# Weight tiles 32 bytes apart and gated features staggered by 16 bytes, in a two-layer hybrid trunk on one core

## The chip, the core and the metric

The kernel runs on one core of a Trainium2 chip. The metric is the device time of one execution in microseconds: the median of several runs. All matrix work is done by TensorE (PE), whose operands both come from SBUF: a *stationary* operand of 128 columns, brought in by a weight load (PEld), and a *moving* operand, streamed past it column by column. VectorE (DVE), ScalarE (ACT) and GpSimd (POOL) do the rest, SyncE (SP) issues the loads.

## The reference, cut to what matters

Two layers, each a mixer (differential attention, latent attention, a state space branch, three gates) and a gated feed-forward network, on 512 tokens of 1024 features in fp32. Nearly all arithmetic is in products like these:

```python
proj = h @ w_in[l]                       # 1024 x 8112
merged = ga * (ya @ w_branch_a[l]) + gb * (yb @ w_branch_b[l]) + gc * (ys @ w_branch_c[l])
x = x + g_m * (merged @ w_out[l])
u = _causal_dwconv(h @ ffn_w_up[l], ffn_conv_w[l], ffn_conv_b[l])   # 1024 x 5632
ua, uv = jnp.split(u, 2, axis=-1)
x = x + g_f * ((jax.nn.silu(ua) * uv) @ ffn_w_down[l])              # 2816 x 1024
```

## The kernel before, in words

Every large product is computed from split operands. A factor is written as a high part, rounded to the matmul's fp32r type, and a low part, the remainder; three matmuls (high with high, high with low, low with high) add up in PSUM. `mm3` (line 140) is that triple: line 141 has the high weights stationary and the high features moving, line 142 the same weights and the low features, line 143 the low weights and the high features. So the weights that are loaded are high, high, low, and so on.

Weights arrive by DMA as a raw tile `wr` of four blocks of 128 rows by 256 columns (1024 fp32 numbers in each partition). `split` (line 126) makes the high part `wh` on ScalarE (line 132) and the low part `wl` on VectorE (line 133), each in a tile of 1024 numbers. The pool `wp` holds three buffers each of `wr`, `wh` and `wl`, so weights are prepared up to some groups ahead. Some groups take `wh` and `wl` from other pools (`wo`, `wd`, `wx`), where a stage needs more of them at once.

`feat_groups` (line 156) is the usual loop: for four blocks of rows at a time it prepares the weights and then issues 4 x 2 triples, two blocks of 128 output features side by side, each over all 512 tokens. `feat_halves` does the same with the tokens in two halves of 256, for the stretches where a norm sits between two products. `tok_groups` (line 192) turns the roles round: the features are stationary and the weights move, 256 columns at a time (lines 220 to 222).

The moving or stationary features are `hh`, `hl` (normed input of a stage, 8 blocks of 512 tokens each), `yh`, `yl` (branch outputs), `mh`, `ml` (merged branches) and `gh`, `gl` (gated features of the feed-forward network, line 1437). In `Ffn.run` (line 1424) the up-product is computed in two parts, of 12 and 10 blocks of 128 features. For each block the gated value `u` is split into `gh` and `gl`, tiles of 512 numbers out of 13 buffers each; then the down-product runs over the blocks of that part with `gh`, `gl` as the moving operand, the second part partly in halves.

The order of the instructions on each engine comes from the program's own order and a scheduler, and the change leaves it as it is on all five. What the pools decide besides the waits is where a tile lies: a pool is laid out tile after tile along the partition, and a tile's length sets where the next begins.

Of the kernel before, what the change touches and what calls it, by code (L numbers as in the profile page):

```python
# [10 lines left out]
F32R = mybir.dt.float32r  # L11
# [7 lines left out]
P = 128  # L19
S = 512  # L20
# [45 lines left out]
def trunk_kernel(ctx: ExitStack, tc: tile.TileContext, a: dict, out: bass.AP):  # L66
# [4 lines left out]
    wp = ctx.enter_context(tc.tile_pool(name="wp", bufs=3, reuse_waits="tile"))  # L71
# [52 lines left out]
        return raw  # L124

    def split(raw, n, scales=None, pool=None):
        hi = (pool or wp).tile([P, 1024], F32R, name="wh")
        lo = (pool or wp).tile([P, 1024], F32R, name="wl")
        for o, m, col in scales or ((0, n, None),):
            sl = slice(o, o + m)  # L130
            if col is None:
                nc.scalar.activation(hi[:, sl], raw[:, sl], AF.Copy)  # L132
                nc.vector.tensor_tensor(out=lo[:, sl], in0=raw[:, sl], in1=hi[:, sl], op=ALU.subtract)  # L133
            else:
                nc.scalar.activation(hi[:, sl], raw[:, sl], AF.Copy, scale=col)
                nc.vector.scalar_tensor_tensor(out=lo[:, sl], in0=raw[:, sl], scalar=col, in1=hi[:, sl],
                                               op0=ALU.mult, op1=ALU.subtract)
        return hi, lo
# [17 lines left out]
    def feat_groups(w, cols, nk, rhs, evac):  # L156
# [5 lines left out]
        def group(k0):  # L162
            n = min(4, nk - k0)

            def prep():
                rows = w[k0 * P:(k0 + n) * P, :].rearrange("(k p) c -> p k c", p=P)
                if joined:
                    raw = load([(0, (n, 256), rows[:, :, cols[0]:cols[0] + 256])])
                    view = "p (k i c) -> p i k c"
                else:  # L170
                    raw = load([(i * n * P, (n, P), rows[:, :, c:c + P]) for i, c in enumerate(cols)])
                    view = "p (i k c) -> p i k c"
                wh, wl = split(raw, n * 256)
                bg(2)
                return [x[:, 0:n * 256].rearrange(view, k=n, i=2) for x in (wh, wl)]

            def mm(weights):
                vh, vl = weights
                if k0 == 0:
                    st["banks"] = [mbank(), mbank()]  # L180
                for k in range(n):
                    xh, xl = rhs(k0 + k)
                    for i in range(2):
                        mm3(st["banks"][i], vh[:, i, k], vl[:, i, k], xh, xl, k0 + k == 0, k0 + k == nk - 1)
                    if k0 + k == nk - 1:
                        for i in range(2):
                            evac(i, st["banks"][i])
                    yield 1.28
            return prep, mm
        return [group(k0) for k0 in range(0, nk, 4)]  # L190

    def tok_groups(w, segs, hh, hl, evac):
# [5 lines left out]
        def group(half):  # L198
            def prep():
                rows = w[half * 512:(half + 1) * 512, :].rearrange("(k p) c -> p k c", p=P)  # L200
                raw = wp.tile([P, 1024], F32, name="wr", bufs=3)
                rv_, off = raw[:, 0:4 * width].rearrange("p (k c) -> p k c", k=4), 0
                for c, n in segs:
                    nc.sync.dma_start(out=rv_[:, :, off:off + n], in_=rows[:, :, c:c + n])
                    off += n
                return split(raw, 4 * width)

            def mm(weights):
                wh, wl = weights
                if half == 0:  # L210
                    st["banks"] = [mbank().rearrange("p (t c) -> p t c", t=2) for _ in range(2)]
                for t in range(T):
                    bank = st["banks"][t // 2]
                    o = bank[:, t % 2, 0:width]
                    ts_ = slice(t * P, (t + 1) * P)
                    first, last = half == 0 and t % 2 == 0, half == 1 and t % 2 == 1
                    for k in range(4):
                        kk = 4 * half + k
                        sl = slice(k * width, (k + 1) * width)
                        nc.tensor.matmul(o, hh[:, kk, ts_], wh[:, sl], start=first and k == 0, stop=False)  # L220
                        nc.tensor.matmul(o, hh[:, kk, ts_], wl[:, sl], start=False, stop=False)  # L221
                        nc.tensor.matmul(o, hl[:, kk, ts_], wh[:, sl], start=False, stop=last and k == 3)  # L222
                    if last:
                        evac(t // 2, bank)
                    yield 1.28
            return prep, mm
# [4 lines left out]
    def feat_halves(w, cols, nk, rhs, evac, joint, pool=None, spare=0):  # L231


        st = {}

        def prep():
            out = []
            for k0 in range(0, nk, 4):
                n = min(4, nk - k0)
                raw = load([(0, (n, 256), w[k0 * P:(k0 + n) * P, cols[0]:cols[0] + 256].rearrange("(k p) c -> p k c", p=P))])  # L240
                out.append([x[:, 0:n * 256].rearrange("p (k i c) -> p i k c", k=n, i=2) for x in split(raw, n * 256, None, pool if nk - k0 <= 4 * spare else None)])
            return out

        def mm(weights, h):
            if h == 0 or not joint:
                st["banks"] = [mbank(), mbank()]
            for k in range(nk):
                vh, vl = weights[k // 4]
                xh, xl = rhs(k)
                for i in range(2):  # L250
                    o = st["banks"][i][:, HALF[h]]
                    mm3(o, vh[:, i, k % 4], vl[:, i, k % 4], xh[:, HALF[h]], xl[:, HALF[h]], k == 0, k == nk - 1)
                if k == nk - 1 and not (joint and h == 0):
                    for i in range(2):
                        if joint:
                            evac(i, st["banks"][i])
                        else:
                            evac(i, st["banks"][i][:, HALF[h]], HALF[h])
                yield 0.64
        return prep, mm  # L260
# [91 lines left out]
    def lin_feat(*args):  # L352
        run_groups(feat_groups(*args))
# [388 lines left out]
    def mix(l, x, hh, hl, ckr, cq, latp, scope):  # L742
# [258 lines left out]
        with ExitStack() as att:  # L1001
# [210 lines left out]
            for h in range(2):  # L1212
                for nm in ("qn", "kn"):
                    mla_transpose(0, h, nm)
            fill(MLA_HEAD[1])
            run(units, events, lambda u: MLA_FILL[u // 8] * MLA_SHAPE[u % 4], (2, 3))
            fill()
            yb = []
# [176 lines left out]
    class Ffn:  # L1395
# [28 lines left out]
        def run(self, fp, extra):  # L1424

            l, x = self.l, self.x
            last = []
            for p0, p1 in ((0, 12), (12, NPAIR)):
                gs = []
                for p2 in range(p0, p1, 2):  # L1430
                    for side in range(2):
                        if (p2, side) != (0, 0):
                            lin_feat(*self.up_args(p2, side))
                    for i in range(2):
                        u = self.us[0, i]
                        nc.vector.tensor_tensor(out=u, in0=u, in1=self.us[1, i], op=ALU.mult)
                        gh = fp.tile([P, S], F32R, name="gh", bufs=13)
                        gl = fp.tile([P, S], F32R, name="gl", bufs=13)
                        nc.scalar.activation(gh, u, AF.Copy)
                        nc.vector.tensor_tensor(out=gl, in0=u, in1=gh, op=ALU.subtract)  # L1440
                        gs.append((gh, gl))
                for n2 in range(4):
                    def evac(i, bank, sl=slice(0, S), n2=n2):
                        n = 2 * n2 + i
                        nc.vector.scalar_tensor_tensor(out=x[:, n, sl], in0=bank, scalar=mod[l][:, 40 + n:41 + n], in1=x[:, n, sl],
                                                       op0=ALU.mult, op1=ALU.add)
                    args = (a["ffn_w_down"][l][p0 * P:p1 * P, :], (n2 * 256, n2 * 256 + P), p1 - p0, lambda k, gs=gs: gs[k], evac)
                    if p0 == 0 or n2 < 2:
                        lin_feat(*args)
                    else:  # L1450
                        last.append(feat_halves(*args, False, extra, 3 * (n2 - 2)))
            return last
# [72 lines left out]
    for l in range(DEPTH):  # L1525
# [13 lines left out]
        fp = np_scope.enter_context(tc.tile_pool(name=f"ffn{l}", bufs=1, reuse_waits="tile"))  # L1539
# [41 lines left out]
```

## Time and profile before

| | |
|---|---|
| time, median of 3 runs (lowest to highest) | 2087.01 us (2086.53 to 2087.76) |
| the profiled execution: its own time | 2087.19 us |
| its span in the profile | 2085.2 us |
| PE busy | 2060.7 us (99% of the span) |
| DVE, ACT, POOL busy | 1415.1, 923.4, 136.0 us |
| HBM traffic | 113 GB/s over the span |

The profile has about 2 us less than the execution's own time: what lies before the first and after the last instruction. A matmul's record begins when it starts and lasts longer than the time to the next one, since matmuls are pipelined: of two successive records the starts tell the pace, and the records' own length does not. A weight load runs beside the matmul before the one that it is for.

### The profile page before, as it was taken

How to read it: one execution, taken by the hardware profiler on the slowest of the kernel's cores; microseconds unless marked ns; L12 is line 12 of the kernel's file. 1: busy time of each engine (PE TensorE's matmuls, PEld its weight loads, DVE VectorE, ACT ScalarE, POOL GpSimd, SP SyncE). 2: the span in 40 equal slices, each digit the busy share in tenths (PEclk: the TensorE clock that was granted, in tenths of full speed). 3: DMA queues.
4: the chain of work that ended last, by engine and by line, in shares of the span. 5: the costliest groups of instructions: out<-in, count | busy, mean ns of one | idle time of the engine just before them, and what ended most of it. 6: DMA issues, size and time to landing. Idle time of an engine off the chain costs nothing.

```text
span 2085.2 us, 30158 instructions
## 1 busy us (share of the span) xinstructions
PE 2060.7 (99%) x11469; PEld 1794.4 (86%) x11469; DVE 1415.1 (68%) x2731; ACT 923.4 (44%) x1702; POOL 136.0 (7%) x162
## 2 busy tenths in 40 slices
PE   8999999999999999999999999999999999999999
PEld 7889988899888988888898888889998888888888
DVE  7788887747876778657767887765566566553553
ACT  6744445535533444224344544454444334432431
POOL 4200011002100000000000000110020000000000
PEclk8999999999999999999999999999999999999999
DMA  8523232243455265655443222212333242323322
GB/s 268 154 61 92 71 117 86 86 123 105 143 157 171 85 189 171 193 175 159 156 136 91 71 61 88 64 48 79 95 89 93 91 132 91 101 91 96 97 91 81
DMA packets 224542, 237.20 MB, mean 114 GB/s; under 512 B 16126, under 2 KB 195742, under 8 KB 224142
## 3 DMA queue, kind: packets, MB, share of 16 engines
q1 hardware_dynamic: 221646, 232.63, 36.5%
q0 software_dynamic: 2752, 2.65, 0.5%
q8 instruction: 90, 1.47, 0.3%
q14 instruction: 54, 0.44, 0.1%
HBM read 226.30 MB, written 8.91 MB: 113 GB/s over the span
## 4 chain that ended last, share of the span: by engine, by line
PE 85%; DVE 5%; issue 5%; DMA 2%; POOL 1%; ACT 1%; SPq 0%; POOLq 0%; DVEq 0%; ACTq 0%
PE mb L141 20%; PE mb L142 20%; PE mb L143 20%; PE mb L220 3%; PE mb L222 3%; PE mb L221 3%; PE ab L1168 2%; PE mb L662 1%; PE ab L1136 1%; DMA wg<-in_ada_w_dram 1%; DVE wl L133 1%; PE ab L961 1%; DVE macc L518 1%; PE ab L1319 1%; PE ab L1078 1%
## 5 line engine op out<-in xcount | busy, mean ns | idle before, releaser
L141 PE MATMUL mb<-hh,wh 128*128 128x512 f32 (+1 forms) x1376 | 538.5, 392 | 2.9 <-DVE modsum L530 1.4
L143 PE MATMUL mb<-hh,wl 128*128 128x512 f32 (+1 forms) x1376 | 532.9, 387 | 0.0
L142 PE MATMUL mb<-hl,wh 128*128 128x512 f32 (+1 forms) x1376 | 532.5, 387 | 0.0
L133 DVE TENSOR_TENSOR wl<-wr,wh 128x1024 fp32r<-128x1024 f32 (+2 forms) x312 | 375.2, 1204 | 201.2 <-ACT wh L132 195.5
L132 ACT ACTIVATE wh<-wr 128x1024 fp32r<-128x1024 f32 (+2 forms) x312 | 324.5, 1041 | 337.3 <-PE mb L142 257.4
L141 PEld LDWEIGHTS mb<-hh,wh 128*128 128x128 f32 x1376 | 258.6, 188 | 53.4 <-DVE modsum L530 2.6
L143 PEld LDWEIGHTS mb<-hh,wl 128*128 128x128 f32 x1376 | 258.7, 188 | 51.4
L142 PEld LDWEIGHTS mb<-hl,wh 128*128 128x128 f32 x1376 | 259.0, 188 | 49.0 <-DVE hl L698 1.2
L1416 DVE SCALAR_TENSOR_TENSOR fu<-mb,vec,fu 128x510 f32<-128x510 f32 (+1 forms) x176 | 129.9, 746 | 91.2 <-ACT fu L1414 89.6
L220 PE MATMUL mb<-wh,hh 128*128 128x256 f32 x640 | 182.4, 285 | 0.0
L221 PE MATMUL mb<-wl,hh 128*128 128x256 f32 x640 | 181.2, 283 | 0.0
L222 PE MATMUL mb<-wh,hl 128*128 128x256 f32 x640 | 181.2, 283 | 0.0
L141 PE MATMUL mb<-gh,wh 128*128 128x512 f32 (+1 forms) x432 | 152.3, 353 | 0.0
L143 PE MATMUL mb<-gh,wl 128*128 128x512 f32 (+1 forms) x432 | 151.7, 351 | 0.0
L142 PE MATMUL mb<-gl,wh 128*128 128x512 f32 (+1 forms) x432 | 151.7, 351 | 0.0
L1414 ACT ACTIVATE fu<-mb,vec 128x512 f32<-128x512 f32 x88 | 67.7, 772 | 149.0 <-PE mb L143 149.0
L220 PEld LDWEIGHTS mb<-wh,hh 128*128 128x128 f32 x640 | 122.6, 192 | 0.8 <-ACT wh L132 0.4
L221 PEld LDWEIGHTS mb<-wl,hh 128*128 128x128 f32 x640 | 122.6, 192 | 0.4
L222 PEld LDWEIGHTS mb<-wh,hl 128*128 128x128 f32 x640 | 122.6, 192 | 0.0
L518 DVE SCALAR_TENSOR_TENSOR macc<-wg,c_act,macc 128x512 f32<-128x512 f32 x140 | 104.8, 749 | 22.9 <-DMA wg<-in_ada_w_dram 22.3
L141 PE MATMUL mb<-yh,wh 128*128 128x512 f32 x256 | 105.4, 412 | 0.9 <-ACT g L765 0.9
L142 PE MATMUL mb<-yl,wh 128*128 128x512 f32 x256 | 101.2, 395 | 0.0
(334 smaller groups left out, 3427.4 us busy)
## 6 DMA issues: line engine op xcount, KB each, us to landing
wr<-in_w_in_dram SPq DMA_DIRECT2D x88, 512.0 KB
wr<-in_ffn_w_up_dram SPq DMA_DIRECT2D x88, 512.0 KB
wg<-in_ada_w_dram SPq DMA_DIRECT2D x160, 256.0 KB
wr<-in_ffn_w_down_dram SPq DMA_DIRECT2D x40, 512.0 KB
wr<-in_w_in_dram SPq DMA_DIRECT2D x64, 256.0 KB
wm<-in_ada_w_dram SPq DMA_DIRECT2D x16, 512.0 KB
wr<-in_w_branch_c_dram SPq DMA_DIRECT2D x16, 512.0 KB
wr<-in_w_out_dram SPq DMA_DIRECT2D x16, 512.0 KB
```

The source lines that it names most:

```text
L132: nc.scalar.activation(hi[:, sl], raw[:, sl], AF.Copy)
L133: nc.vector.tensor_tensor(out=lo[:, sl], in0=raw[:, sl], in1=hi[:, sl], op=ALU.subtract)
L141: nc.tensor.matmul(o, lh, rh, start=first, stop=False)
L142: nc.tensor.matmul(o, lh, rl, start=False, stop=False)
L143: nc.tensor.matmul(o, ll, rh, start=False, stop=last)
L220: nc.tensor.matmul(o, hh[:, kk, ts_], wh[:, sl], start=first and k == 0, stop=False)
L221: nc.tensor.matmul(o, hh[:, kk, ts_], wl[:, sl], start=False, stop=False)
L222: nc.tensor.matmul(o, hl[:, kk, ts_], wh[:, sl], start=False, stop=last and k == 3)
L518: ins = nc.vector.scalar_tensor_tensor(out=acc[0], in0=rk, scalar=c_act[:, kk:kk + 1], in1=acc[0], op0=ALU.mult, op1=ALU.add)
L1168: nc.tensor.matmul(po[:, t * P:n], vv[:, j], st["pT"][:, j * P:(j + 1) * P], start=j == 0, stop=j == t)
L1414: nc.scalar.activation(u, bank, AF.Identity, bias=v[:, V_FCB + ti:V_FCB + ti + 1], scale=tap(2))
L1416: nc.vector.scalar_tensor_tensor(out=u[:, s_:], in0=bank[:, 0:S - s_], scalar=tap(2 - s_), in1=u[:, s_:], op0=ALU.mult, op1=ALU.add)
```

## The change

The tiles `wh` become 1024 + 8 numbers long, of which the first 1024 are used as before. The tiles `gh` and `gl` become 512 + 8 numbers long, and the gated features stand in the first 512 of them for every even block of a part and four numbers further on for every odd one.

```diff
     def split(raw, n, scales=None, pool=None):
-        hi = (pool or wp).tile([P, 1024], F32R, name="wh")
+        hi = (pool or wp).tile([P, 1024 + 8], F32R, name="wh")
         lo = (pool or wp).tile([P, 1024], F32R, name="wl")
...
-                        gh = fp.tile([P, S], F32R, name="gh", bufs=13)
-                        gl = fp.tile([P, S], F32R, name="gl", bufs=13)
+                        at = 4 * (len(gs) % 2)
+                        gh, gl = [fp.tile([P, S + 8], F32R, name=nm, bufs=13)[:, at:at + S] for nm in ("gh", "gl")]
```

No instruction is added, removed or moved. What differs is the place of tiles within a partition. The table gives where they start, in bytes modulo 128 (the blocks inside a tile follow at multiples of 512 bytes, so the same holds for them, except in the latent product of 432 columns):

| tile | before | after |
|---|---|---|
| `hh`, `hl` | 64 | 64 |
| `wh` in `wp`, buffers 1, 2, 3 | 64, 64, 64 | 64, 96, 0 |
| `wl` in `wp`, all three | 64 | 32 |
| `yh`, `yl`, `mh`, `ml` | 0 | 96 |
| `gh`, `gl` | 0 | all multiples of 32, and of 32 plus 16 in odd blocks |
| `wh`, `wl` in `wo` (last quarter of the output product) | 96, 96 | 64, 96 |
| `wh`, `wl` in `wd` (last quarter of the first layer's down-product) | 64, 64 | 96 or 0 or 32, 64 |

## Rows read from the trace of the kernel before

**Rows 1.** The page, parts 1 and 2: busy time, share and instructions of each engine; busy tenths of PE and the granted clock of PE in 40 slices of the span.

```profile
PE 2060.7 (99%) x11469; PEld 1794.4 (86%) x11469; DVE 1415.1 (68%) x2731; ACT 923.4 (44%) x1702; POOL 136.0 (7%) x162
PE   8999999999999999999999999999999999999999
PEclk8999999999999999999999999999999999999999
```

**Rows 2.** What PE waited for, by line and releaser, longest in total first: us in total, times, longest.

```profile
PE ab L620 <- DVE hdiff L600: 4.3, 1, 4.3
PE ab L472 <- DMA c<-in_c_dram: 2.4, 1, 2.4
...
PE mb L295 <- ACT wh L132: 1.4, 1, 1.4
```

**Rows 3.** Groups of PE instructions by line and shape: line, engine, operation, output<-moving,stationary, shapes, count | busy us, mean ns of one | idle before them.

```profile
L141 PE MATMUL mb<-hh,wh 128*128 128x512 f32 x1312 | 520.2, 397 | 2.1 <-DVE modsum L530 1.4 <-DVE g L774 0.7
L220 PE MATMUL mb<-wh,hh 128*128 128x256 f32 x640 | 182.4, 285 | 0.0
L141 PE MATMUL mb<-gh,wh 128*128 128x512 f32 x272 | 107.6, 396 | 0.0
L141 PE MATMUL mb<-yh,wh 128*128 128x512 f32 x256 | 105.4, 412 | 0.9 <-ACT g L765 0.9
L141 PE MATMUL mb<-gh,wh 128*128 128x256 f32 x160 | 44.7, 279 | 0.0
L141 PE MATMUL mb<-mh,wh 128*128 128x256 f32 x128 | 36.0, 281 | 0.0
L141 PE MATMUL mb<-mh,wh 128*128 128x512 f32 x64 | 25.3, 395 | 0.0
L141 PE MATMUL mb<-hh,wh 128*128 128x256 f32 x64 | 18.7, 292 | 0.8 <-ACT hh L697 0.8
```

**Rows 4.** The timeline of PE in the second layer's up-product (moving `hh`, `hl`, 512 columns): start us, length us, engine, line, operation. The last row is the 27th after the first.

```profile
1950.11 0.39 PE L141 MATMUL mb<-hh,wh 128*128 128x512 f32 x1
1950.34 0.39 PE L142 MATMUL mb<-hl,wh 128*128 128x512 f32 x1
...
1956.23 0.39 PE L141 MATMUL mb<-hh,wh 128*128 128x512 f32 x1
```

**Rows 5.** The same for the second layer's down-product (moving `gh`, `gl`, 512 columns). The last row is the 27th after the first.

```profile
1850.39 0.40 PE L141 MATMUL mb<-gh,wh 128*128 128x512 f32 x1
1850.62 0.39 PE L142 MATMUL mb<-gl,wh 128*128 128x512 f32 x1
...
1856.69 0.40 PE L141 MATMUL mb<-gh,wh 128*128 128x512 f32 x1
```

**Rows 6.** The same for a branch product (moving `yh`, `yl`) and for the output product (moving `mh`, `ml`), 512 columns each. Of each pair of rows the second is the 27th after the first.

```profile
1622.52 0.40 PE L142 MATMUL mb<-yl,wh 128*128 128x512 f32 x1
...
1628.82 0.39 PE L142 MATMUL mb<-yl,wh 128*128 128x512 f32 x1
...
1666.49 0.40 PE L141 MATMUL mb<-mh,wh 128*128 128x512 f32 x1
...
1672.79 0.39 PE L141 MATMUL mb<-mh,wh 128*128 128x512 f32 x1
```

**Rows 7.** The same in `tok_groups` (moving `wh`, `wl`, 256 columns, stationary `hh`, `hl`). The last row is the 27th after the first.

```profile
1436.10 0.28 PE L221 MATMUL mb<-wl,hh 128*128 128x256 f32 x1
...
1439.35 0.28 PE L221 MATMUL mb<-wl,hh 128*128 128x256 f32 x1
```

**Rows 8.** The same in the first layer's down-product in halves of 256 columns: two rows of the first half, then two of the second half, under the norm's work. Of each pair the second is the 27th after the first.

```profile
1054.19 0.28 PE L141 MATMUL mb<-gh,wh 128*128 128x256 f32 x1
...
1057.25 0.28 PE L141 MATMUL mb<-gh,wh 128*128 128x256 f32 x1
...
1074.92 0.28 PE L141 MATMUL mb<-gh,wh 128*128 128x256 f32 x1
...
1078.10 0.28 PE L141 MATMUL mb<-gh,wh 128*128 128x256 f32 x1
```

**Rows 9.** The same in the first layer's output product in halves, where the stationary weights pass from the pool `wp` to `wo` at 693.3 us, the moving tile being the same. The second row is the 9th after the first, the fourth the 23rd after the third.

```profile
692.13 0.28 PE L143 MATMUL mb<-mh,wl 128*128 128x256 f32 x1
...
693.15 0.28 PE L143 MATMUL mb<-mh,wl 128*128 128x256 f32 x1
...
693.51 0.28 PE L143 MATMUL mb<-mh,wl 128*128 128x256 f32 x1
...
696.27 0.28 PE L142 MATMUL mb<-ml,wh 128*128 128x256 f32 x1
```

**Rows 10.** The timeline of PE and PEld in the second layer's up-product: a matmul, and the weight load that starts beside it for the matmul behind it.

```profile
1949.88 0.39 PE L143 MATMUL mb<-hh,wl 128*128 128x512 f32 x1
1949.89 0.19 PEld L141 LDWEIGHTS mb<-hh,wh 128*128 128x128 f32 x1
```

**Rows 11.** Groups of ACT and DVE instructions that write the tiles which the change moves, by line and shape; columns as in rows 3.

```profile
L132 ACT ACTIVATE wh<-wr 128x1024 fp32r<-128x1024 f32 x296 | 312.3, 1056 | 327.8 <-PE mb L142 247.9 <-issue 40.2 <-PE mb L222 35.2
L1439 ACT ACTIVATE gh<-fu 128x512 fp32r<-128x512 f32 x44 | 27.6, 627 | 60.0 <-DVE fu L1436 60.0
...
L133 DVE TENSOR_TENSOR wl<-wr,wh 128x1024 fp32r<-128x1024 f32 x296 | 361.5, 1222 | 200.9 <-ACT wh L132 195.1 <-DMA wg<-in_ada_w_dram 1.8 <-PE mb L143 1.5
L1440 DVE TENSOR_TENSOR gl<-fu,gh 128x512 fp32r<-128x512 f32 x44 | 30.2, 687 | 0.5
```

## The prediction

> **What bounds the kernel now.** I read the busy times first: PE works in 99% of the span, and from the third slice of forty on at the full clock [rows 1]. The waits come next: the longest that PE has is 4.3 us, once, at the start, and what it waits for a weight tile is 1.4 us, once [rows 2]. So time is won or lost in the pace of the matmuls alone, and the third view is the one that matters: the timeline of PE, where successive starts give the pace and the records' lengths do not.
>
> In the up-product 27 matmuls of 512 columns take 1956.23 - 1950.11 = 6.12 us, 226.7 ns each [rows 4]. In the down-product, the same shape at the same clock, 27 take 6.30 us, 233.3 ns each [rows 5]; branch and output products pace at 233.3 ns as well [rows 6]. With 256 columns it is the other way round: weights moving past `hh` take 3.25 / 27 = 120.4 ns [rows 7], gated features 3.06 / 27 = 113.3 ns [rows 8]. The paces stand on rungs about 6.7 ns apart, the time of 16 columns at 2.4 GHz.
>
> What tells these groups apart is where the tiles lie. Call *distance* the start of the stationary block less that of the moving one, modulo 128 bytes. By the table of places it is 0 in rows 4 and 7 and 64 in rows 5, 6 and the rest. Distance 0 goes with the lower rung at 512 columns and the higher one at 256, distance 64 the reverse. That the stationary side has a part shows in one product: its moving tile stays, its weights pass from distance 64 to 96, and the pace goes from 1.02 / 9 = 113.3 to 2.76 / 23 = 120.0 ns [rows 9]. The weight load of the next matmul starts 10 ns after the matmul before it [rows 10], so both reads run side by side; I take the rungs for what the two cost each other. That is inferred: no row shows a read being held up.
>
> **The change part by part.** It adds no instruction and moves none. ScalarE and VectorE write the displaced tiles as often as before, 1056 and 1222 ns for a weight tile and 627 and 687 ns for a gated one [rows 11]. If places changed these, what covers it is the weight buffers ahead: one group of four blocks is 24 matmuls or 24 x 0.227 = 5.4 us of PE, against 2.3 us for making its two tiles. I cost it at nothing; without that cover each tile's excess would be paid on PE. What is left is five terms, each a number of matmuls by a change of rung. After the change the distance differs within one triple, since high and low weights lie differently.
>
> *Up-products and all others on `hh`, `hl`, 512 columns:* 3 x 1312 = 3936 matmuls [rows 3], now all at distance 0. After: 880 stay at 0, 848 are at 32, 896 at 64, 1312 (those with `wl`) at 96. Distance 64 is known, 233.3 instead of 226.7 ns: 896 x 6.67 = +6.0 us. For 96 the one row is of 256 columns, and there 96 has the rung that 0 has [rows 7, 9]; I take it for 512 columns too, so 0. No row has 32: between nothing and one rung, I take half, 848 x 3.33 = +2.8 us. Bounds: one rung less for each that leaves distance 0 and isn't known to lose, (848 + 1312) x -6.67 + 6.0 = -8.4 us; one more for each, 3056 x 6.67 = +20.4 us. Term: **+8.8 us**.
>
> *Weights moving, 256 columns:* 3 x 640 = 1920 matmuls [rows 3], all at 0. After: 384 at 0, 384 at 64, 512 at 96, 640 at 32. At 64 they gain a rung, 384 x -6.67 = -2.6 us [rows 7, 8]; 96 as at 0; at 32 half a rung, -2.1 us. Bounds: -2.6 us with a rung gained or lost by each of the other 1152, so -10.3 to +5.1 us. Term: **-4.7 us**.
>
> *Branch and output products, 512 columns:* 3 x (256 + 64) = 960 [rows 3], all at 64. After: 320 stay, 192 are at 0, 224 at 96, 224 at 32: 416 x -6.67 and 224 x -3.33 = **-3.5 us**. Bounds: -1.3 us (only distance 0 gains) and -4.3 us (all 640 that leave distance 64 gain).
>
> *Down-products, 512 columns:* 3 x 272 = 816 [rows 3], all at 64. After they are spread evenly over the multiples of 16. With the four known or assumed places (a rung at 0 and 96, half at 32, none at 64) the mean is -4.2 ns: **-3.4 us**. Places with the odd 16 appear in no row; bounds are 0 and one rung for each, -5.4 us.
>
> *Halves of 256 columns:* 480 on `gh`, 384 on `mh`, 192 on `hh` [rows 3]. The first two are mostly at distance 64, which is best here, but only in the first half: in the second, beside the norm's work, the pace is 3.18 / 27 = 117.8 ns anyway [rows 8]. So about 400 lose 3 to 4 ns and the `hh` ones gain a little: **+1.3 us**, between 0 and +2.9 us (432 x 6.67).
>
> The sum is 8.8 - 4.7 - 3.5 - 3.4 + 1.3 = -1.5 us. The profiled execution took 2087.2 us, so 2085.7; the median is 0.2 lower: **2085.5 us**. All of it is a balance of gains and losses several times as large.
>
> At this place the Trainium skill speaks against any effect. SBUF — State Buffer, "Who interferes with whom", gives PE two read ports, one for the moving operand and one for weight loads, independent of each other, and says that PE never waits for anyone; by that the sum would be 0. The trace disagrees in so far as the same shape paces at 226.7 and 233.3 ns [rows 4, 5], and at 113.3 and 120.0 ns past one and the same moving tile [rows 9].
>
> **The rivals.**
>
> *Only equal places are good for 512 columns (slower).* The place is the products on `hh`, where distance 0 holds for thousands of matmuls in a row. If any other distance costs the rung, all 3056 that leave it go to 233.3 ns: +20.4 us; with the mirror image at 256 columns (only 64 gains, -2.6 us; halves +2.9) and 192 + about 100 gains in the other products (-1.9 us) it is +18.8 us, **2106 us**. It decides as soon as more than half of the 2160 matmuls at 32 and 96 lose a rung. For it: all three groups of 512 columns away from distance 0 have the same 233.3 ns [rows 5, 6]. Against: only one other distance has been seen there.
>
> *Spreading undoes the collisions (faster).* If it is the unbroken repetition of one distance that costs, then with distances changing from matmul to matmul the lower rung is had everywhere and `hh` keeps it: 1776 matmuls of 512 columns from 233.3 to 226.7, -11.8 us, and most of 1920 of 256 columns from 120 to 113.3, up to -12.8 us, so about -20 us after some loss in the halves: **2067 us**. For it: at 256 columns both rungs occur, so the higher is no law of the shape [rows 7, 8]. Against: in the second halves, with the same places, the pace is neither rung but 117.8 ns [rows 8], so other work unsettles the pace as well and settles it in between.
>
> *It does not do what it says.* If the rungs come from something other than the distance, such as the product's kind or what the other engines do, nothing moves: **2087 us**. Rows 9 speak against it.
>
> **How the numbers follow.** The balance gets 0.40, with a range of its own of 2078 to 2093 (two of the half-rung choices wrong in the same direction). The loss of equal places gets 0.25, the gain of spreading 0.25, no effect 0.10. About 0.2% (4.2 us) is what a measurement of this kernel can tell from no change. Of the balance 0.15 lies more than that below, 0.17 within and 0.08 above. So faster 0.15 + 0.25 = 0.40, within 0.17 + 0.10 = 0.27, slower 0.08 + 0.25 = 0.33. A range of 2064 to 2106 us takes in the balance, most of both rivals and their bounds, and leaves out somewhat under 0.2.
>
> **What would show it.** The waits of PE stay under a few us and the number of instructions is the same. In the up-product's timeline the pace should differ from one group of 24 matmuls to the next, with the buffer of `wh`: about 227 ns with the first buffer, and towards 231 with the third. The down-product should fall from 233.3 to about 229 ns, the weights-moving products from 120.4 to about 118 ns. The balance is wrong if the up-product's mean pace is over 231 ns (first rival) or at or under 227 ns (second), and all of it is wrong if the paces are as before.

## The result: slower by 0.7%, and the profile after

| | before | after |
|---|---|---|
| time, median (lowest to highest), 4 runs each on the same chip | 2087.39 us (2086.53 to 2088.62) | 2102.44 us (2101.99 to 2103.89) |
| span of the profiled execution | 2085.2 us | 2100.4 us |

The ratio is 1.0068, with a 95% interval of 1.0056 to 1.0081. The time lies inside the range of the prediction, but 17 us above its forecast of 2085.5 us, and further from the time before than the 4.2 us that it took for no change.

First the busy times and instructions of the engines after (to be read beside [rows 1]).

```profile
PE 2076.0 (99%) x11469; PEld 1795.6 (85%) x11469; DVE 1416.2 (67%) x2731; ACT 924.8 (44%) x1702; POOL 136.4 (6%) x162
```

The instructions are the same, PE again fills 99% of the span, and its busy time has grown by 15.3 us; those of the engines that write the displaced tiles by 1.1 and 1.4 us. Next, what PE waited for after, by line and releaser: us in total, times, longest (beside [rows 2]).

```profile
PE ab L620 <- DVE hdiff L600: 3.7, 1, 3.7
PE mb L662 <- DVE st L651: 3.3, 4, 1.9
...
PE mb L295 <- ACT wh L132: 1.0, 1, 1.0
```

No new wait. So the time went where the prediction looked for it, into the pace of the matmuls. The groups of PE instructions by shape after (columns as in [rows 3]) show which:

```profile
L141 PE MATMUL mb<-hh,wh 128*128 128x512 f32 x1312 | 526.6, 402 | 1.6 <-DVE g L774 1.3 <-DVE modsum L530 0.3
L220 PE MATMUL mb<-wh,hh 128*128 128x256 f32 x640 | 180.7, 282 | 0.0
L141 PE MATMUL mb<-gh,wh 128*128 128x512 f32 x272 | 107.3, 394 | 0.0
L141 PE MATMUL mb<-yh,wh 128*128 128x512 f32 x256 | 104.9, 410 | 1.0 <-ACT g L765 1.0
L141 PE MATMUL mb<-gh,wh 128*128 128x256 f32 x160 | 45.3, 283 | 0.0
```

The products on `hh` rise by 6.4 us on line 141 alone; weights moving, down-products and branch products at 512 columns fall a little; the halves rise. The timeline of PE in the second layer's up-product after (beside [rows 4]; the last row is the 27th after the first):

```profile
1963.27 0.39 PE L141 MATMUL mb<-hh,wh 128*128 128x512 f32 x1
1963.51 0.39 PE L142 MATMUL mb<-hl,wh 128*128 128x512 f32 x1
1963.74 0.40 PE L143 MATMUL mb<-hh,wl 128*128 128x512 f32 x1
...
1969.53 0.39 PE L141 MATMUL mb<-hh,wh 128*128 128x512 f32 x1
```

It is 6.26 / 27 = 231.9 ns, where [rows 4] had 226.7. The branch product (beside [rows 6]) and the weights moving (beside [rows 7], here in the first layer) come to such middle paces from the other side: 6.26 / 27 = 231.9 ns from 233.3, and 3.19 / 27 = 118.1 ns from 120.4.

```profile
1631.11 0.40 PE L142 MATMUL mb<-yl,wh 128*128 128x512 f32 x1
...
1637.37 0.40 PE L142 MATMUL mb<-yl,wh 128*128 128x512 f32 x1
```

```profile
429.26 0.28 PE L221 MATMUL mb<-wl,hh 128*128 128x256 f32 x1
...
432.45 0.28 PE L221 MATMUL mb<-wl,hh 128*128 128x256 f32 x1
```

Both traces hold the same matmuls in the same order, so the times from each start to the next can be summed by kind, over the whole trace:

| kind (matmuls) | before, us | after, us | difference |
|---|---|---|---|
| on `hh`, `hl`, 512 columns (3936) | 915.0 | 930.4 | +15.5 |
| weights moving, 256 (1920) | 231.3 | 227.9 | -3.4 |
| branch and output, 512 (960) | 229.1 | 227.8 | -1.3 |
| down, 512 (816) | 190.6 | 189.4 | -1.3 |
| halves, 256 (1056) | 126.0 | 128.9 | +2.9 |
| the first 75 us of the span | 72.8 | 75.6 | +2.8 |
| all others (2430) | 313.7 | 313.7 | 0.0 |

It adds up to 15.2 us, the difference of the spans. The five kinds of split products make 12.4 us of it; the first 75 us are taken up under what stays open. The kernel has lost its lower rungs: on the mean of a triple, products of 512 columns now pace at 231 to 232 ns and those of 256 at about 118 ns. Single steps still differ: in the second layer's up-product the three steps of a triple take 235.6, 231.7 and 226.7 ns with the third buffer of `wh`.

### The profile page after: what moved, and what is told of

It reads as the page before. It is cut to its first block, busy times and chain, and to the rows that moved or that the text cites. A ratio compares the mean times of both kernels' runs of the same rounds, so it can differ in the third digit from the quotient of the medians.

```text
span 2100.4 us, 30158 instructions
## 1 busy us (share of the span) xinstructions
PE 2076.0 (99%) x11469; PEld 1795.6 (85%) x11469; DVE 1416.2 (67%) x2731; ACT 924.8 (44%) x1702; POOL 136.4 (6%) x162
## 4 chain that ended last, share of the span: by engine, by line
PE 85%; DVE 5%; issue 5%; DMA 2%; POOL 1%; ACT 0%; SPq 0%; POOLq 0%; DVEq 0%; ACTq 0%
PE mb L141 21%; PE mb L142 21%; PE mb L143 21%; PE mb L222 3%; PE mb L220 3%; PE mb L221 3%; PE ab L1168 2%; PE ab L1136 1%; PE ab L961 1%; DMA wg<-in_ada_w_dram 1%; PE ab L1078 1%; DVE macc L518 1%; PE ab L1319 1%; DVE wl L133 1%; PE mb L662 1%
## 5 line engine op out<-in xcount | busy, mean ns | idle before, releaser
L141 PE MATMUL mb<-hh,wh 128*128 128x512 f32 (+1 forms) x1376 | 544.9, 396 | 2.4 <-DVE g L774 1.3
L222 PEld LDWEIGHTS mb<-wh,hl 128*128 128x128 f32 x640 | 120.4, 188 | 0.0
L143 PE MATMUL mb<-yh,wl 128*128 128x512 f32 x256 | 101.0, 394 | 0.0
```

Source lines behind the costliest of these rows:

```text
L141: nc.tensor.matmul(o, lh, rh, start=first, stop=False)
L143: nc.tensor.matmul(o, ll, rh, start=False, stop=last)
```

## The experiments

Two theories stood after the result. **Own distance** (theory O in the expectations): each matmul has the pace of its own distance, and I had the wrong values for 32 and 96. **Mixing** (theory M): a rung is kept only while the distance repeats from one matmul to the next; where it changes inside a triple, the mean pace comes to about 232 or 118 ns. The result alone does not tell them apart: with 233.3 ns at 32 and 64 and 234.3 at 96, own distance gives (880 x 226.7 + 1744 x 233.3 + 1312 x 234.3) / 3936 = 232.2 ns for the products on `hh`, and 232.1 was measured. Paces below are from start to start over long runs of one product, unless two rows are shown. The distance is taken modulo 256 where that matters, for a reason found on the way. All ratios are against the kernel before on the same chip. Edits are shown in short: the parameters `gap` and `off`, which `split` gets for them, are left out.

**The two halves of the change.** The first keeps only the longer `wh`, the second only the places of the gated features.

```diff
-        hi = (pool or wp).tile([P, 1024], F32R, name="wh")
+        hi = (pool or wp).tile([P, 1024 + 8], F32R, name="wh")
```

> Only the 32 bytes between the high weight tiles, the gated features as before. Theory M (mixing: a pace stays on a rung only while the distance between stationary and moving block repeats from matmul to matmul; where it changes from one matmul to the next, 512 columns pace at about 231.6 ns and 256 columns at about 118.2 ns, whatever the distances): products on hh +15 us, weights-moving products -3.4 us, halves +3, branch and output products -1.5, gated ones -1.5, so +12 us, about 2099. Theory O (own distance: each matmul paces by its own distance, and 32 and 96 cost most of a rung at 512 columns): the same within 3 us. If the gated features' stagger is what costs: 2087.

Measured: 2101.17 us, ratio 1.0062 (1.0045 to 1.0079). Timeline of the up-product: 6.27 / 27 = 232.2 ns.

```profile
1923.49 0.39 PE L141 MATMUL mb<-hh,wh 128*128 128x512 f32 x1
...
1929.76 0.39 PE L141 MATMUL mb<-hh,wh 128*128 128x512 f32 x1
```

```diff
-                        gh = fp.tile([P, S], F32R, name="gh", bufs=13)
-                        gl = fp.tile([P, S], F32R, name="gl", bufs=13)
+                        at = 4 * (len(gs) % 2)
+                        gh, gl = [fp.tile([P, S + 8], F32R, name=nm, bufs=13)[:, at:at + S] for nm in ("gh", "gl")]
```

> Only the gated features' part, the weights as before. Products on hh at 226.7 ns and weights-moving products at 120 ns as before. Theory M: high and low features lie at different distances, so down-products fall from 233.3 to about 231.6 ns, 816 x -1.7 = -1.4 us, and their halves rise from 113.3 to about 118, +2 us: 2088, no change. Theory O: some gain at distances 0 and 96, 2085. If the stagger is the cause of the loss: 2100 or more.

Measured: 2088.87 us, ratio 1.0001 (0.9991 to 1.0010). The up-product keeps its rung, 6.15 / 27 = 227.8 ns in the rows below and 226.7 over the long run; the down-product goes from 233.3 to 6.27 / 27 = 232.2, and its halves from 114.2 to 118.1 ns, a loss (1.8 us on all halves) that eats the gain (0.8 us).

```profile
1917.58 0.40 PE L141 MATMUL mb<-hh,wh 128*128 128x512 f32 x1
...
1923.73 0.39 PE L141 MATMUL mb<-hh,wh 128*128 128x512 f32 x1
```

```profile
1850.65 0.39 PE L141 MATMUL mb<-gh,wh 128*128 128x512 f32 x1
...
1856.92 0.40 PE L141 MATMUL mb<-gh,wh 128*128 128x512 f32 x1
```

So the result comes from the weight tiles: the longer `wh` alone costs 12.2 us, about the 12.4 us of the table by kind. The gated features' stagger is worth nothing here.

**Mixing against own distance.** Here `wh` stays at distance 0 to `hh` and only `wl` moves, by 96 bytes, through a tile that is never used. Two of every three matmuls keep distance 0.

```diff
+        gap or gap.append(wp.tile([P, 24], F32, name="gap", bufs=1))   # once, ahead of wl
         lo = (pool or wp).tile([P, 1024], F32R, name="wl")
```

> No stagger between buffers: all high weight tiles stay where they were (distance 0 to hh), and the low ones stand 96 bytes further on, as in the change. Theory M: the distance still changes within each triple, so products on hh pace at about 231.6 ns for all three matmuls, +15 us or more, weights-moving products 118, total about 2099, the same as with the high weights staggered. Theory O: two of three matmuls keep distance 0 and 226.7 ns, the third goes to about 231: +6 us, less 1 for the weights-moving ones, 2091. If the stagger from buffer to buffer is the cause: 2087.

Measured: 2100.86 us, ratio 1.0058 (1.0042 to 1.0075). The timeline of the up-product gives 6.28 / 27 = 232.6 ns.

```profile
1923.32 0.39 PE L141 MATMUL mb<-hh,wh 128*128 128x512 f32 x1
1923.55 0.39 PE L142 MATMUL mb<-hl,wh 128*128 128x512 f32 x1
1923.78 0.39 PE L143 MATMUL mb<-hh,wl 128*128 128x512 f32 x1
1924.01 0.40 PE L141 MATMUL mb<-hh,wh 128*128 128x512 f32 x1
...
1929.60 0.39 PE L141 MATMUL mb<-hh,wh 128*128 128x512 f32 x1
```

Own distance, with 234.3 ns at 96 (measured below), gives (2 x 226.7 + 234.3) / 3 = 229.2. By line the means are 233.4, 231.7 and 232.7 ns for lines 141, 142 and 143: line 141 has distance 0 itself, the load beside it is for a matmul at distance 0, and it is the slowest of the three. So a pace that hangs on a matmul's own distance alone is refuted, and mixing stands.

**All weights moved by one amount.** The unused tile now stands ahead of `wh`, 8, 16 or 24 numbers long, so all weight tiles move together by 32, 64 or 96 bytes and the distance to `hh` is the same again for every matmul of the up-product. These runs give the rung of each distance without mixing.

```diff
+        gap or gap.append(wp.tile([P, 8], F32, name="gap", bufs=1))   # once, ahead of wh; 16 and 24 in the others
         hi = (pool or wp).tile([P, 1024], F32R, name="wh")
```

> All weight tiles, high and low, 32 bytes further on, and the tiles behind them too: the distance to hh is 32 for every matmul, and never changes; to the branch and gated features it stays 64. Theory M: products on hh hold one rung, 226.7 or 233.3 ns, flat, not between; weights-moving products 113.3 or 120 ns, flat. So 2087, 2074, 2113 or 2100 by which rungs. Theory O: about 232 ns and 118 ns, +21 - 4, 2104. Branch, output and gated products stay at 233.3 ns in both.

> All weight tiles, high and low, 64 bytes further on, the tiles behind them too: distance to hh 64 for every matmul, to the other features 64 as before. Theory M (a pace stands on a rung where the distance repeats; which rung is set by that distance and by the number of columns): products on hh 233.3 ns flat, +26 us; weights-moving products 113.3 ns, -12.8 us; so 13 us over the kernel before, about 2101. A rival in which any move of the weight tiles costs the same, whatever the distance: 2105 as with 32 bytes, weights-moving products at about 117.

> The same with 96 bytes, the distance that the change gives to the low weights, here for all and never changing. The prediction took 96 to rank with 0: products on hh 226.7 ns, time as before, 2088. Theory M says only that the pace is flat on a rung: 226.7 or 233.3 ns on hh, so 2088 or 2114, less up to 12.8 us if the weights-moving products fall to 113.3 ns.

| weights moved by | time, us | ratio (95%) | up-product, 512 columns | weights moving, 256 columns |
|---|---|---|---|---|
| 0 (before) | - | 1 | 226.7 ns | 119.8 ns |
| 32 | 2104.74 | 1.0076 (1.0058 to 1.0095) | 233.3 | 116.7 |
| 64 | 2103.97 | 1.0075 (1.0059 to 1.0090) | 233.3 | 117.8 |
| 96 | 2112.14 | 1.0116 (1.0099 to 1.0133) | 234.3 | 119.9 |

The up-product's timelines at 32, 64 and 96 in turn: 6.29, 6.31 and 6.32 us for 27.

```profile
1928.56 0.40 PE L141 MATMUL mb<-hh,wh 128*128 128x512 f32 x1
...
1934.85 0.40 PE L141 MATMUL mb<-hh,wh 128*128 128x512 f32 x1
```

```profile
1923.56 0.40 PE L141 MATMUL mb<-hh,wh 128*128 128x512 f32 x1
...
1929.87 0.39 PE L141 MATMUL mb<-hh,wh 128*128 128x512 f32 x1
```

```profile
1933.33 0.39 PE L141 MATMUL mb<-hh,wh 128*128 128x512 f32 x1
...
1939.65 0.40 PE L141 MATMUL mb<-hh,wh 128*128 128x512 f32 x1
```

Three things follow. At 512 columns only distance 0, of these four, has the lower rung; that 96 ranks with it, which the forecast took from 256 columns, is refuted by the worst pace of the row. These kernels are no faster than the change, and the one at 96 is slower: mixing at 232 ns is no worst case, it lies below the rungs of 32, 64 and 96. And one expectation missed: at 64 bytes the weights-moving products should have come to 113.3 ns and came to 3.18 / 27 = 117.8.

```profile
1442.47 0.28 PE L221 MATMUL mb<-wl,hh 128*128 128x256 f32 x1
...
1445.65 0.28 PE L221 MATMUL mb<-wl,hh 128*128 128x256 f32 x1
```

There the distance is not 64 but -64, since the weights are the moving operand. With a period of 128 the two would be the same place; with 256 they are 64 and 192. The next runs bear on that. But the trace has more than one pace for this distance: two stretches, the same one in either layer, run at 113.3 ns throughout, 3.07 / 27 = 113.7 in these rows.

```profile
1478.18 0.28 PE L220 MATMUL mb<-wh,hh 128*128 128x256 f32 x1
...
1481.25 0.28 PE L220 MATMUL mb<-wh,hh 128*128 128x256 f32 x1
```

**Weights that move at distance 64.** The tiles get 32 numbers (128 bytes) more, and in `tok_groups` the weights stand 16 numbers into them. For room, some small tiles have fewer buffers here and in the two kernels with 256 bytes, and in those two a scratch tile has one buffer less as well.

```diff
-        hi = (pool or wp).tile([P, 1024], F32R, name="wh")
+        hi = (pool or wp).tile([P, 1024 + 32], F32R, name="wh")[:, off:off + 1024]      # wl alike
...
-                return split(raw, 4 * width)
+                return split(raw, 4 * width, off=16)
```

> Weight tiles are 128 bytes longer (which leaves all starts modulo 128 as before; room comes from fewer buffers of eight-number tiles), and in the weights-moving products alone the weights stand 64 bytes into their tile: there distance 64 instead of 0. Theory M: these 1920 matmuls fall from 120 to 113.3 ns, all others keep their rungs: -12.8 us, about 2075. If 128 bytes are not the period, products on hh leave 226.7 ns. If the pace belongs to the kind of product and not to the distance: 2088.

Measured: 2099.06 us, ratio 1.0051 (1.0035 to 1.0067): a miss of 24 us and of the sign. The weights-moving products came to 117.7 ns, and the up-product, whose places modulo 128 had not moved, fell off its rung: 6.24 / 27 = 231.1 ns in these rows, 232.0 over the long run.

```profile
1919.98 0.39 PE L141 MATMUL mb<-hh,wh 128*128 128x512 f32 x1
...
1926.22 0.39 PE L141 MATMUL mb<-hh,wh 128*128 128x512 f32 x1
```

A tile longer by 128 bytes puts every other buffer at distance 128. If the period were 128 nothing would mix. So either it is longer, or the tiles' length or the fewer buffers are what costs. The counter-test lengthens the tiles of `wp` by 64 numbers, 256 bytes:

```diff
-        hi = (pool or wp).tile([P, 1024], F32R, name="wh")
+        hi = (pool or wp).tile([P, 1024 if pool else 1024 + 64], F32R, name="wh")[:, off:off + 1024]   # wl alike
```

> Weight tiles 256 bytes longer instead of 128 (room from fewer small buffers and one buffer less of a scratch tile), all starts modulo 256 as before, nothing stands into its tile. After the run with 128 bytes longer tiles, in which products on hh left their rung, Theory M needs 256 bytes as the period, the 128 having made two distances that alternate. Then all rungs are as before: hh 226.7 ns, weights-moving 120 ns, 2088. If any lengthening of the weight tiles (another spacing of the three buffers) is what costs: hh at 232 ns and 2100. If the period is 512: the same 2100.

Measured: 2088.22 us, ratio 1.0000 (0.9990 to 1.0010), and every pace as before: 226.7 ns in the up-product (6.14 / 27 = 227.4 in these rows), 119.8 with weights moving, 233.3 in the down-product.

```profile
1916.90 0.39 PE L141 MATMUL mb<-hh,wh 128*128 128x512 f32 x1
...
1923.04 0.39 PE L141 MATMUL mb<-hh,wh 128*128 128x512 f32 x1
```

So neither longer tiles as such nor the fewer buffers do it, and the places that matter in the up-product repeat at 256 bytes and not at 128.

**The features at distance 0.** If distance 0 is good at 512 columns, the other products should be given it. The unused tile of 16 numbers stands behind `wl`, and all features but `hh`, `hl` move by 64 bytes.

```diff
         lo = (pool or wp).tile([P, 1024], F32R, name="wl")
+        gap or gap.append(wp.tile([P, 16], F32, name="gap", bufs=1))   # once, behind wl
```

> A gap of 64 bytes behind the weight tiles, so that branch, merged and gated features lie at distance 0 to the weights instead of 64; the products on hh are untouched. Theory M: 960 + 816 matmuls of 512 columns fall from 233.3 to 226.7 ns, -11.8 us; their halves of 256 columns rise from 113.3 (or 118) to 120 ns, +3.5 us: -8 us, about 2080. If the rung belongs to the kind of product: 2088.

Measured: 2082.90 us, ratio 0.9975 (0.9965 to 0.9984). The down-product comes from 233.3 to 226.7 ns (6.11 / 27 = 226.3 in these rows), the output product to the same, the branch product to 228.8; the halves pay with 119.9 ns, as distance 0 has it at 256 columns. The direction and the paces are those expected; the time gained is 5.7 us where 8 were expected.

```profile
1843.82 0.39 PE L141 MATMUL mb<-gh,wh 128*128 128x512 f32 x1
...
1849.93 0.39 PE L141 MATMUL mb<-gh,wh 128*128 128x512 f32 x1
```

**Distances chosen by shape.** Weight tiles of `wp` longer by 256 bytes, as in the counter-test; one small tile with a buffer more than there, which moves the features by 64 bytes to distance 0; and in `tok_groups` and the halves the weights stand 192 and 64 bytes into their tiles, so that products of 256 columns have distance 64 modulo 256 where they can.

```diff
-                return split(raw, 4 * width)
+                return split(raw, 4 * width, off=48)
...
-                out.append([... for x in split(raw, n * 256, None, pool if nk - k0 <= 4 * spare else None)])
+                out.append([... for x in split(raw, n * 256, None, pool if nk - k0 <= 4 * spare else None, 0 if nk - k0 <= 4 * spare else 16)])
```

> As with 256 bytes longer weight tiles, and each product gets the distance with the lower rung, counted modulo 256 and never changing within it: 512 columns at distance 0 (branch, merged and gated features 64 bytes on, as in the run with features at 0), weights-moving products and halves at 64 (weights 192 or 64 bytes into their tile; the run with all weights 64 bytes on had 192 there, and 117.5 ns). Theory M: 1776 matmuls of 512 columns -6.67 ns, -11.8 us; 1920 of 256 columns from 120 to 113.3 ns, -12.8 us; halves about 0: 2064. If 113.3 ns belongs to gated and merged features only: 2076.

Measured: 2073.91 us, ratio 0.9928 (0.9914 to 0.9941), 0.7% faster than before and the fastest of all kernels here, though 10 us short of what was expected. The 512-column products pace at 226.7 ns, the branch product at 228.8 as in the run before. The weights-moving products reach 113.3 ns in eight of the ten stretches of 96 or more (3.07 / 27 = 113.7 in the rows below) and hold 3.18 / 27 = 117.8 in the other two, the same stretch in either layer (10.0 us saved in all, against 12.8 if it were 113.3 throughout). The halves of the down-product come to 117.6 where they stand at 64, not to 113.3, and to 119.9 where they stand at 0. The time lies near the 2076 of the other expectation, that 113.3 ns belongs to gated and merged features only; the pace of the eight stretches refutes that.

```profile
158.78 0.28 PE L220 MATMUL mb<-wh,hh 128*128 128x256 f32 x1
...
161.96 0.28 PE L220 MATMUL mb<-wh,hh 128*128 128x256 f32 x1
...
1426.10 0.28 PE L221 MATMUL mb<-wl,hh 128*128 128x256 f32 x1
...
1429.17 0.28 PE L221 MATMUL mb<-wl,hh 128*128 128x256 f32 x1
```

## Why the prediction was wrong

**What held.** The bound is the pace of PE, no wait appeared, the writers of the moved tiles cost nothing that PE sees, and the places of the tiles decide the pace. The rival by which nothing moves is out.

**The step that failed** is the first term, *all others on `hh`, `hl`, 512 columns*: +8.8 us forecast, +15.5 measured. It failed in three ways.
- It priced each matmul by its own distance. But 880 matmuls that stay at distance 0 were costed at nothing, and in a triple with `wl` at 96 the mean pace leaves their rung. In the second layer's up-product after, the three starts of a triple take 697.3 ns with the first buffer of `wh` (own distances 0, 0, 96), 696.9 with the second (32, 32, 96) and 694.0 with the third (64, 64, 96), so 232.4, 232.3 and 231.3 ns a matmul. The forecast was 227 with the first and towards 231 with the third: the first is the slowest. The kernel that moves `wl` against `wh` shows that this is mixing and not a wrong table. The mean hides unlike steps: those of the third buffer take 235.6, 231.7 and 226.7 ns, and the one at the lower rung is the matmul on `wl` at distance 96.
- It let 96 rank with 0, from one row at 256 columns [rows 9]. At 512 columns it has the worst rung, 234.3 ns. A rank was carried from one shape to another.
- It counted the distance modulo 128. In the up-product 0 and 128 are different places, as the two lengthened kernels show; the distances of this term are the same either way, but in the weights-moving products, where the sign turns, the 64, 96 and 32 of the prediction are 192, 224 and 160 modulo 256, and a remedy that goes by the places modulo 128 goes wrong.

**The other terms** had the right sign. Three gains were put too large: -3.4 us with weights moving (forecast -4.7), -1.3 in branch and output products (-3.5), -1.3 in the down-products (-3.4). The loss in the halves was put too small: +2.9 us, its upper bound, against +1.3. Each assumed that matmuls at a good distance reach the lower rung. After the change few do: of the 3936 on `hh`, 2695 started their successor in under 228 ns before and 291 after.

**The rivals.** "Only equal places are good for 512 columns" had the sign, the place and nearly the size: 2106 us against 2102.4, and the sign set for it, a mean pace over 231 ns in the up-product, came. The nearness is in part luck: the paces show 12.4 of its 18.8 us, and 2.8 us of the start, which it did not forecast, make up part of the rest. Its rule is right for distances that repeat (32, 64 and 96 all cost a rung), but in the change itself the distances do not repeat, and what is paid there is the mixed pace, a mean of 232 ns a matmul, whatever the distances of the triple. Its term on `hh` was +20.4 us, and 15.5 came: the mixed pace is 1 to 2 ns better than the upper rung, and part of the matmuls were not on the lower rung before. "Spreading undoes the collisions" is refuted: what changes from matmul to matmul paces on the mean near the upper rung, not at the lower. Its counter-argument, the 117.8 ns of [rows 8], is close to the 118 ns that mixing gives at 256 columns, but nothing mixes there: the distance is 64 throughout.

I had the evidence that should have turned the balance, and weighed it too lightly: three groups away from distance 0 all had the upper rung [rows 5, 6], and the half rung for 32 and the rank of 96 stood against that on one row of another shape.

The Trainium skill's rule, in SBUF — State Buffer, "Who interferes with whom", that the two read ports of PE are independent and PE waits for no one, would have given no change. The runs disagree: changing the places of tiles alone, with every instruction the same, gives ratios from 1.0058 to 1.0116.

**What stays open.** The first 75 us take 2.8 us more after the change. The traces show that this stretch varies anyway: the first product of split weights starts between 68.4 and 74.9 us in the twelve traces, and in the counter-test with 256 bytes, whose paces are all as before, it starts later than after the change. Its rows from before, after and the counter-test:

```profile
69.63 0.44 PE L295 MATMUL mb<-wh,hh 128*128 128x432 f32 x1
...
72.32 0.44 PE L295 MATMUL mb<-wh,hh 128*128 128x432 f32 x1
...
73.64 0.44 PE L295 MATMUL mb<-wh,hh 128*128 128x432 f32 x1
```

So the 2.8 us are not shown to come from the change; what the paces show of it is 12.4 us.

Why mixing gives the pace that it does was not found: in the lengthened kernel with 128 bytes, line 141 still paces at 226.7 ns where it stands at distance 0 behind a matmul at 128, and the other steps of such triples at 232 to 235 ns. And the rule of 256 columns is not complete: the same distance of 64 gave 113.3 ns in one place and 117.6 to 117.8 in others, 192 gave both too, and a stretch holds the one or the other from end to end. In the kernel with all weights moved by 32 bytes the first half of the second layer's down-product keeps its distance of 64, since the gated features move along, and goes from 3.06 / 27 = 113.3 ns to 3.18 / 27 = 117.8 (before, then that kernel):

```profile
2051.56 0.28 PE L141 MATMUL mb<-gh,wh 128*128 128x256 f32 x1
...
2054.62 0.28 PE L141 MATMUL mb<-gh,wh 128*128 128x256 f32 x1
...
2070.66 0.28 PE L141 MATMUL mb<-gh,wh 128*128 128x256 f32 x1
...
2073.84 0.28 PE L141 MATMUL mb<-gh,wh 128*128 128x256 f32 x1
```

So something besides the distance modulo 256 has a part there. That the moving read and the weight load disturb each other is the picture that led to these tests; no row shows the disturbance itself.

## What to carry to other kernels

Where PE is busy throughout, read its pace from successive starts and set it beside the places of both operands; groups of one shape with different paces are worth as much as a wait. Lay out the high and low parts so that every matmul in a run has the same distance between its stationary and its moving block, and choose that distance for the shape by a run: here it is 0 for 512 columns, while for 256 columns 64 reached the best pace in some stretches only. A tile that is lengthened for one purpose shifts every buffer behind the first, so pad by a multiple of 256 bytes, which cost nothing in the one run with it, or place the padding outside the rotating buffers.

## What the runs showed of the hardware

- Matmuls of the split products have a pace set by where their operands lie: at 512 columns 226.7 ns for distance 0, 233.3 for 32 and 64, 234.3 for 96, and 231 to 232 on the mean of a triple where the distance changes within it (single steps of the change's up-product 226.7 to 235.6).
- At 256 columns it runs from 113.3 ns (64, in some places) through 116.7 (224) and 117.8 (192, but 113.3 in two stretches) to 119.8 to 120 (0, 96, 160), and is about 118 when mixed. At one distance (64, 192) a stretch holds 113.3 or 117.8 ns from end to end.
- In the up-product the pattern repeats at 256 bytes (2088.22 us, all paces kept) and not at 128 (2099.06 us).
- The choice of places alone moved the whole kernel from 0.9928 to 1.0116 of its time.
